# First weights cut in three, first transfers on two queues, and a written order for the first splits

## The chip, the cores and the metric

The kernel runs on one core of one Trainium2 chip. The metric is the device time of one execution in microseconds. Engines are named as in the profile: PE (TensorE), DVE (VectorE), ACT (ScalarE), POOL (GpSimd), and SP, which here only issues DMAs. Each engine works through its own instructions in the order in which they were built, and waits where one needs a result, or a buffer, of another engine.

## The reference

Two layers of a decoder trunk on x with 512 tokens and 1024 features, in float32. The case touches only the start of the first layer's Conformer module:

```python
u = rms_norm(h, conv_norm_g)                    # h = x
a = u @ w_pw1 + b_pw1                           # 1024 -> 2048
u = a[..., :D_MODEL] * jax.nn.sigmoid(a[..., D_MODEL:])
u = causal depthwise convolution of 31 taps(u) + dw_b
h = h + silu(layer_norm(u)) @ w_pw2 + b_pw2
...
def rms_norm(x, g):
    y = xf * lax.rsqrt(jnp.mean(xf * xf, axis=-1, keepdims=True) + EPS)
    return y * g
```

The rest (SwiGLU, a gated input embedding, differential attention with its own SwiGLU and embedding) is the same code before and after.

## The kernel before

**Layout.** x is held transposed: eight chunks h0 to h7 of 128 features by 512 tokens (256 KB each). A product with a weight is taken in three matmuls, so that float32 comes out of the faster rounded format: each operand is split into a rounded upper part ("hi") and the remainder ("lo"), and lo·hi, hi·hi and hi·lo are summed (`mm3`, lines 163 to 168). A weight tile is 128 x 1024 (512 KB) and holds all eight blocks of 128 x 128 that one chunk of 128 outputs needs. `weight()` (147 to 161) loads it with a DMA from SP into one of two buffers `wraw`, casts it on ACT into `whi` (159) and subtracts on DVE into `wlo` (161). I number these tiles w0, w1, ... in the order in which they are loaded.

**The norm.** The norm's scale per token is left out of the first product and multiplied in behind it. What the matmuls see is h times the gain, split the same way into a tile `A` of which one half is hi (ACT, 206) and one lo (DVE, 207). Meanwhile ACT squares the eight chunks (237); chunks 0 to 2 are summed over the features on PE by matmuls against ones (199), chunk 3's square is the tile `acc`, into which POOL adds the squares of 4 to 7 (241), and `acc` is summed on PE last. From the sums DVE makes a mean (270), POOL an inverse root (272), DVE a diagonal matrix (277), PE spreads it over the partitions (288, output `tp`), and ACT copies it into the row `rb` (262). All products of this stage are multiplied by `rb`.

**The chunk loop** (500 to 549) makes the 16 x 128 outputs in eight chunks. Each takes a gate half and a value half, 24 matmuls of 128 x 512 each, in accumulators `mm`, of which there are four in rotation: chunk 2's gate half writes the one that chunk 0's gate half used. DVE multiplies both halves by `rb` (523, 529), which frees the accumulators; ACT takes the sigmoid (524, with a table load ahead of it), DVE joins the two (541, or 533 for chunks 1, 3, 5, 6, which goes on by DMA through DRAM, 370 and 374, to convolution taps on PE at 407). The taps of chunks 0, 2 and 4 run on DVE (453, 455, 458) and, as products of ACT summed by POOL, on those two (442, 445, 446). Each chunk also loads the next chunk's two weights, so w2 and w3 serve chunk 1, w4 and w5 chunk 2, w6 and w7 chunk 3. Between w5 and w6 two halves of the input p use the same two `wraw` buffers (312 to 314; ACT casts, POOL subtracts). A buffer's next transfer is issued by SP when its cast and its subtraction are done, so w4 follows w2, p's first half follows w4, and w6 follows p's first half.

**The order** of the instructions on each engine is set by the building program's scheduler, except where the code binds it (`issue_after`, and `manual_schedule` for whole blocks). The first two weights come in two halves each, with the first chunks of x between them on SP's queue (lines 299 to 307). Only `vec`, a table of gains and biases, comes by ACT's queue (120).

Of the kernel before, what the change touches and what calls it, by code (L numbers as in the profile page):

```python
# [13 lines left out]
F32R = mybir.dt.float32r  # L14
# [32 lines left out]


SHIFT = 1
WARM = 9  # L50
ALONE = (7,)
CUTS = 2

# [38 lines left out]
def trunk(ctx, tc, xT, pT, wts, diag, dww, vec, rel, onehot, lamv, out):  # L92
# [9 lines left out]
    def sb(shape, tag, bufs, dt=F32):  # L102
        uid[0] += 1
        return pool.tile(shape, dt, tag=tag, name=f"{tag}_{uid[0]}", bufs=bufs)
# [12 lines left out]


    vt = sb([P, 480], "vec", 1)[:, :NV]
    nc.scalar.dma_start(vt, vec)  # L120

    def col(name, i=0):
        a, _ = VEC[name]
# [8 lines left out]
    V.memset(mhalf, -0.5)  # L132
    V.memset(meps, DH * EPS)
    t = wk()[:, 0:P]
    V.memset(t, 1.0)
    V.tensor_copy(ones_r, t)

# [9 lines left out]
    def weight(n=1024, pieces=1, between=(), eng=V, after=(None, None), home=None, parts=None, bufs=1):  # L147
        i = wnext[0]
        wnext[0] += 1
        raw = sb([P, 1024], *(home or ("wraw", 2)))  # L150
        hi = sb([P, 1024], *((parts[0], bufs) if parts else ("whi", 4)), F32R)
        lo = sb([P, 1024], *((parts[1], bufs) if parts else ("wlo", 4)), F32R)
        for k in range(pieces):
            cut = slice(k * n // pieces, (k + 1) * n // pieces)
            loaded[0] = nc.sync.dma_start(raw[:, cut], wts[i, :, cut])
            if k < len(between):
                between[k]()
            with tc.issue_after(after[1].ins) if after[1] else nullcontext():
                A.copy(hi[:, cut], raw[:, cut])  # L159
            with tc.issue_after(after[0].ins) if after[0] else nullcontext():  # L160
                eng.tensor_tensor(lo[:, cut], raw[:, cut], f(hi[:, cut]), ALU.subtract)  # L161
        return hi, lo
# [27 lines left out]
        return t[:, 0], t[:, 1]  # L190


    h = [sb([P, S], f"h{c}", 1) for c in range(NC)]

    def columns_sum(t, src, first, last):

        for b in range(4):
# [11 lines left out]
    class Norm:  # L209
# [18 lines left out]
                self.square = A.activation(sq, h[c], AF.Square)  # L228
                self.last = self.eng.tensor_tensor(self.acc, self.acc, sq, ALU.add)  # L229

        def columns_of_chunks(self, n):

            t = tp()
            acc = sb([P, S], "acc", 1)
            for c in range(NC):
                sq = wk() if c != n else acc
                A.activation(sq, h[c], AF.Square)
                if c < n:
                    columns_sum(t, sq, c == 0, False)
                elif c > n:  # L240
                    G.tensor_tensor(acc, acc, sq, ALU.add)
            columns_sum(t, acc, False, True)
            return rsqrt_cols(first_of(t), 4, 1.0 / D)
# [49 lines left out]


    norm = Norm("conv_g")
    def load(c):
        return lambda: nc.sync.dma_start(h[c], xT[c])

    w0 = weight(pieces=2, between=(load(0),))
    norm.split(0)  # L300
    w1 = weight(pieces=2, between=(load(1), load(2)))
    pair_loads = [loaded[0]]
    pairs = [(w1, w0)]
    for c in range(3, NC):
        load(c)()
    for c in range(1, NC):
        norm.split(c)

    def pfeatures(layer, parts):
        for k, (hi, lo) in enumerate(parts):  # L310
# [189 lines left out]
    for c in range(NC):  # L500
        wa, wg = pairs[c]
        if c == 0:
            pg = half(wg)
            pa = half(wa)
            norm.dg = diagonal(norm.columns_of_chunks(3))
            rb = norm.rows()
        if c + 1 < NC:
            pairs.append((weight(), weight())[::-1])
            pair_loads.append(loaded[0])
        if c == 0:  # L510
            dwt = sb([P, NC * KW], "C4", 2)
            nc.sync.dma_start(dwt, dww)
        if c == 1:
            ph = pfeatures(0, [(sb([P, S], t, 2, F32R), sb([P, S], t, 2, F32R)) for t in ("wth", "wtl")])
        if c > 0:
            pg = half(wg)
            for k in BETWEEN[c]:
                pe_taps(k)
            pa = half(wa)
            for k in BEHIND[c]:  # L520
                pe_taps(k)
        tg, ta = big(), big()
        V.tensor_tensor(tg, pg, rb, ALU.mult)
        gated = A.activation(tg, tg, AF.Sigmoid, bias=col("b_pw1", 8 + c))
        if c == NC - 1:

            with tc.issue_after(gated.ins):
                A.activation(powers[:, 24:32], vt[:, :8], AF.Silu)
        V.tensor_tensor(ta, pa, rb, ALU.mult)
        if c in PHASED:  # L530
            up = big()
            phases, tok = "p (r n) -> p n r", "p (n r) -> p n r"
            V.scalar_tensor_tensor(
                up.rearrange(phases, r=NPH), ta.rearrange(tok, r=NPH), col("b_pw1", c),
                tg.rearrange(tok, r=NPH), ALU.add, ALU.mult,
            )
            phased_in(c, up)
        else:
            up = ups[c] = sb([P, S + PAD], "C0", 2)
            G.memset(up[:, :PAD], 0.0)  # L540
            V.scalar_tensor_tensor(up[:, PAD:], ta, col("b_pw1", c), tg, ALU.add, ALU.mult)
        for k in BETWEEN[c] + BEHIND[c]:
            other_taps(k)
        if c == 1:
            moments(0)
        elif c > 3:
            moments(c - 3)
# [862 lines left out]
```

## Time and profile before

| | us |
|---|---|
| median of 3 runs | 1246.81 (1246.58 to 1248.63) |
| the profiled execution | 1246.42 |
| its span, first to last instruction | 1244.70 |
| around the span | 1.72 |
| PE busy | 1232.4 (99% of the span) |
| DVE, ACT, POOL busy | 882.1, 623.8, 471.1 |

Times in rows of the profile count from the span's start. A row of the timeline gives the start, the length, the engine, the line of the kernel, the operation, output and inputs, how many instructions were merged, and in brackets how long the engine stood idle before it and whose result ended that. "SPq" and "ACTq" are DMA issues of SP and ACT. PE's matmuls overlap, so that one of 0.39 us is followed by the next after 0.23. A float32 matmul with "ones" shows as two passes. "PEclk", the clock that the throttle granted, is full in every slice of the page.

### The profile page before, as it was taken

Reading aid. Unit: us, or ns where it says so; the run is one execution under the profiler, and the core shown is the slowest. Engines: PE = TensorE matmul, PEld = TensorE weight load, DVE = VectorE, ACT = ScalarE, POOL = GpSimd, SP = SyncE. Lnnn points to the kernel's source line nnn. Section 1 sums busy time; section 2 is a strip of 40 time slices with the busy share of each in tenths; the row PEclk is TensorE's granted clock in tenths of the full one; section 3 lists DMA queues with packets and bytes.
Section 4 is the critical chain, followed back from the end, with each engine's and each line's share of the span. In section 5 each row is a group of like instructions: output and inputs, shape, how many; then the busy total and the mean of one; then the engine's idle time right before and its main releaser. Section 6 shows DMA issues by size and latency. Waiting matters only on the chain.

```text
span 1244.7 us, 18430 instructions
## 1 busy us (share of the span) xinstructions
PE 1232.4 (99%) x7080; PEld 1080.8 (87%) x7080; DVE 882.1 (71%) x1242; ACT 623.8 (50%) x1096; POOL 471.1 (38%) x355
## 2 busy tenths in 40 slices
PE   9999999999999999999999999999999999999998
PEld 7888788888998899888888888788889998999887
DVE  6998866885895479547676876646966885587535
ACT  5653464443553255434566877735434552455432
POOL 3863442024670364133346645041026650552120
PEclk9999999999999999999999999999999999999999
DMA  7566213334233322334332331143333333232331
GB/s 267 177 210 193 90 51 119 98 98 127 86 102 118 102 86 71 117 104 149 126 113 76 112 90 38 52 144 93 89 122 95 103 111 112 83 102 86 104 100 67
DMA packets 49154, 136.33 MB, mean 110 GB/s; under 512 B 5635, under 2 KB 10243, under 8 KB 49068
## 3 DMA queue, kind: packets, MB, share of 16 engines
q1 hardware_dynamic: 46944, 131.74, 34.0%
q10 hardware_dynamic: 2124, 3.43, 0.9%
q8 instruction: 55, 0.90, 0.3%
q14 instruction: 31, 0.25, 0.1%
HBM read 128.84 MB, written 6.31 MB: 109 GB/s over the span
## 4 chain that ended last, share of the span: by engine, by line
PE 88%; DVE 4%; issue 2%; DMA 1%; ACT 0%; SPq 0%; POOL 0%; DVEq 0%; ACTq 0%
PE mm L166 27%; PE mm L167 27%; PE mm L168 27%; PE mm L1126 1%; DVE sc L458 1%; PE sc L1094 1%; PE sc L1093 1%; PE tp L1113 1%; PE sc L407 1%; PE mm L407 1%; PE tp L1047 1%; PE mm L363 1%; PE tp L199 1%; DVE wlo L720 0%; DVE wlo L161 0%
## 5 line engine op out<-in xcount | busy, mean ns | idle before, releaser
L159 ACT CAST whi<-wraw 128x1024 fp32r<-128x1024 f32 (+2 forms) x145 | 145.7, 1014 | 229.0 <-PE mm L168 110.9
L161 DVE TENSOR_TENSOR wlo<-wraw,whi 128x1024 fp32r<-128x1024 f32 (+2 forms) x141 | 180.4, 1285 | 82.0 <-ACT whi L159 79.7
L166 PE MATMUL mm<-A,wlo 128*128 128x512 f32 (+1 forms) x568 | 220.4, 388 | 1.1 <-ACT A L206 1.0
L167 PE MATMUL mm<-A,whi 128*128 128x512 f32 (+1 forms) x568 | 219.2, 387 | 0.0
L168 PE MATMUL mm<-A,whi 128*128 128x512 f32 (+1 forms) x568 | 217.3, 389 | 0.0
L166 PE MATMUL mm<-B,wlo 128*128 128x512 f32 x352 | 137.0, 389 | 0.0
L167 PE MATMUL mm<-B,whi 128*128 128x512 f32 x352 | 137.0, 389 | 0.0
L168 PE MATMUL mm<-B,whi 128*128 128x512 f32 x352 | 135.6, 389 | 0.0
L229 POOL TENSOR_TENSOR acc<-acc,wk 128x512 f32<-128x512 f32 x35 | 60.0, 1715 | 190.6 <-ACT wk L228 189.9
L166 PEld LDWEIGHTS mm<-A,wlo 128*128 128x128 f32 x568 | 106.8, 188 | 23.7 <-ACT A L206 1.3
L167 PE MATMUL mm<-C,whi 128*128 128x256 f32 x448 | 126.8, 283 | 0.0
L168 PE MATMUL mm<-C,whi 128*128 128x256 f32 x448 | 126.8, 283 | 0.0
L166 PE MATMUL mm<-C,wlo 128*128 128x256 f32 x448 | 126.8, 283 | 0.0
L168 PEld LDWEIGHTS mm<-A,whi 128*128 128x128 f32 x568 | 106.5, 188 | 21.9 <-issue 0.5
L167 PEld LDWEIGHTS mm<-A,whi 128*128 128x128 f32 x568 | 106.7, 188 | 21.1
L720 DVE TENSOR_TENSOR wlo<-A,whi 128x1024 fp32r<-128x1024 f32 x60 | 106.2, 1778 | 19.7 <-ACT whi L719 19.6
L719 ACT CAST whi<-A 128x1024 fp32r<-128x1024 f32 x60 | 62.9, 1049 | 55.5 <-PE mm L168 44.3
L729 POOL TENSOR_TENSOR A<-A 128x512 f32<-128x512 f32 x16 | 25.7, 1606 | 165.5 <-DMA A<-in_wts 156.7
L729 POOL TENSOR_TENSOR A<-wraw 128x512 f32<-128x512 f32 x16 | 24.7, 1546 | 167.4 <-DMA wraw<-in_wts 152.7
L167 PEld LDWEIGHTS mm<-C,whi 128*128 128x128 f32 x448 | 86.0, 192 | 0.2
L166 PEld LDWEIGHTS mm<-C,wlo 128*128 128x128 f32 x448 | 86.0, 192 | 0.2
L168 PEld LDWEIGHTS mm<-C,whi 128*128 128x128 f32 x448 | 86.0, 192 | 0.0
(314 smaller groups left out, 3031.6 us busy)
## 6 DMA issues: line engine op xcount, KB each, us to landing
wraw<-in_wts SPq DMA_DIRECT2D x161, 512.0 KB, 3.6
A<-in_wts SPq DMA_DIRECT2D x32, 512.0 KB, 3.6
wraw<-in_wts SPq DMA_DIRECT2D x16, 384.0 KB, 3.1
D<-in_diag SPq DMA_DIRECT2D x22, 256.0 KB, 4.8
C<-in_diag SPq DMA_DIRECT2D x16, 256.0 KB, 4.8
h<-in_xT SPq DMA_DIRECT2D x8, 256.0 KB, 5.5
rest<-h SPq DMA_DIRECT2D x8, 256.0 KB, 2.5
bias<-scr ACTq DMA_DIRECT2D x8, 256.0 KB, 3.6
```

The source lines that it names most:

```text
L159: A.copy(hi[:, cut], raw[:, cut])
L161: eng.tensor_tensor(lo[:, cut], raw[:, cut], f(hi[:, cut]), ALU.subtract)
L166: T.matmul(acc, al, bh, start=first, stop=False, **kw)
L167: T.matmul(acc, ah, bh, start=False, stop=False, **kw)
L168: return T.matmul(acc, ah, bl, start=False, stop=last, **kw)
L199: r = T.matmul(t[:, cut], src[:, cut], ones, start=first and b == 0, stop=last and b == 3)
L229: self.last = self.eng.tensor_tensor(self.acc, self.acc, sq, ALU.add)
L363: last_tap[0] = T.matmul(acc, dg[:, j % 4], ups[c][:, j : j + S], start=(j == 0), stop=(j == PE_TAPS[c] - 1))
L407: last_tap[0] = T.matmul(acc[:, g * P : (g + 1) * P], w, ups[c][:, g, LEAD - m : LEAD - m + P], start=(m == 0), stop=(m == LAGS - 1),)
L719: A.copy(hi, src)
L720: V.tensor_tensor(lo, src, f(hi), ALU.subtract)
L729: G.tensor_tensor(s[:, 0], r1[:, 0], r1[:, 1], ALU.add)
```

## The change

It does five things. (1) The tile h0 is issued first on SP, then `vec` on ACT as before, and the warm-up matmuls before the first data are 7 instead of 9. (2) w0 and w1 are cut into pieces of 256, 256 and 512 columns instead of 512 and 512; the first two pieces of w0 are issued from ACT's queue, all else from SP's, with h1, h2 and h3 between the pieces. (3) The casts, subtractions, the eight splits of x and the squares of chunks 0 to 3 stand in a written order for DVE and ACT. (4) The squares of chunks 0 to 3 are passed to the norm's column sums (`squares`), and the others are left to the scheduler. (5) In chunk 0 the gate and value halves are written as one loop over the eight blocks, six matmuls each.

```diff
-WARM = 9
+WARM = 7
...
-    nc.scalar.dma_start(vt, vec)
...
+    h = [sb([P, S], f"h{c}", 1) for c in range(NC)]
+    nc.sync.dma_start(h[0], xT[0])
+    nc.scalar.dma_start(vt, vec)
...
-        def columns_of_chunks(self, n):
+        def columns_of_chunks(self, n, given):
...
-            acc = sb([P, S], "acc", 1)
+            acc = given[n]
             for c in range(NC):
-                sq = wk() if c != n else acc
-                A.activation(sq, h[c], AF.Square)
+                if c in given:
+                    sq = given[c]
+                else:
+                    sq = wk()
+                    A.activation(sq, h[c], AF.Square)
...
-    w0 = weight(pieces=2, between=(load(0),))
-    norm.split(0)
-    w1 = weight(pieces=2, between=(load(1), load(2)))
-    pair_loads = [loaded[0]]
+    pieces = slice(0, 256), slice(256, 512), slice(512, 1024)
...
+    def fetch(i, k, eng):
+        return eng.dma_start(raw2[i][:, pieces[k]], wts[i, :, pieces[k]])
+
+    fetch(0, 0, nc.scalar)
+    fetch(1, 0, nc.sync)
+    fetch(0, 1, nc.scalar)
+    load(1)
+    fetch(1, 1, nc.sync)
+    load(2)
+    fetch(0, 2, nc.sync)
+    load(3)
+    pair_loads = [fetch(1, 2, nc.sync)]
     pairs = [(w1, w0)]
-    for c in range(3, NC):
-        load(c)()
-    for c in range(1, NC):
-        norm.split(c)
+    for c in range(4, NC):
+        load(c)
...
+    with tc.manual_schedule(engines={V.engine, A.engine}):
+        whi(0, 0)
+        wlo(0, 0)
+        norm.split(0)
+        whi(1, 0)
+        norm.split(1)
+        wlo(1, 0)
...
+        norm.split(7)
+        square(3)
...
         if c == 0:
-            pg = half(wg)
-            pa = half(wa)
-            norm.dg = diagonal(norm.columns_of_chunks(3))
+            pg, pa = mm(), mm()
+            for k in range(NC):
+                (gh, gl), (ah, al), (bh, bl) = wpart(wg, k), wpart(wa, k), norm.u[k]
+                T.matmul(pg, gl, bh, start=k == 0, stop=False)
+                T.matmul(pg, gh, bh, start=False, stop=False)
+                T.matmul(pa, ah, bh, start=k == 0, stop=False)
+                T.matmul(pg, gh, bl, start=False, stop=k == NC - 1)
+                T.matmul(pa, ah, bl, start=False, stop=False)
+                T.matmul(pa, al, bh, start=False, stop=k == NC - 1)
+            norm.dg = diagonal(norm.columns_of_chunks(3, squares))
             rb = norm.rows()
```

Where it moves instructions: the scheduler lays out the rest around the written part, and its order differs from before until chunk 4's gate half; from there on all engines have the same order. Three places follow, each as built. In the rows a name's last number tells tiles apart.

On ACT at the start, before (`whi_96` and `whi_109` are the upper parts of w0 and w1, `A_18`, `A_22`, `A_23` the splits of chunks 0 to 2, `wk` their squares):

```order
L120 DMA vec_63<-in_vec 128x99
L159 ACT_TABLE_LOAD
L159 CAST whi_96<-wraw_95 128x512
L206 ACTIVATE A_18_105<-h_7_87,vec_63 128x512
L237 ACTIVATE wk_199<-h_7_87 128x512
L159 CAST whi_96<-wraw_95 128x512
L159 CAST whi_109<-wraw_108 128x512
L206 ACTIVATE A_22_124<-h_8_88,vec_63 128x512
L237 ACTIVATE wk_205<-h_8_88 128x512
L159 CAST whi_109<-wraw_108 128x512
L206 ACTIVATE A_23_127<-h_9_89,vec_63 128x512
```

And now (`whi_96` and `whi_98` are w0 and w1, `A_21` to `A_23` the splits):

```order
L136 DMA vec_63<-in_vec 128x99
L308 DMA wraw_94<-in_wts 128x256 x2
L330 ACT_TABLE_LOAD
L330 CAST whi_96<-wraw_94 128x256
L206 ACTIVATE A_21_117<-h_6_74,vec_63 128x512
L330 CAST whi_98<-wraw_95 128x256
L206 ACTIVATE A_22_121<-h_7_75,vec_63 128x512
L330 CAST whi_96<-wraw_94 128x256
L330 CAST whi_98<-wraw_95 128x256
L206 ACTIVATE A_23_128<-h_8_76,vec_63 128x512
L327 ACTIVATE wk_132<-h_6_74 128x512
```

Two DMA issues came to ACT, the first casts are half as long, and the first square moved behind the splits of chunks 0 to 2.

On PE at the end of chunk 1, before (`mm_316` is chunk 1's value half, `tp_241<-wk_238` the matmul that spreads rb, `A_22` and `A_23` the splits of chunks 1 and 2 of the eight):

```order
L166 MATMUL mm_316<-A_22_124,wlo_252 128x512
L167 MATMUL mm_316<-A_22_124,whi_251 128x512
L288 MATMUL tp_241<-wk_238,ones_70 128x512
L168 MATMUL mm_316<-A_22_124,whi_251 128x512
L166 MATMUL mm_316<-A_23_127,wlo_252 128x512
L167 MATMUL mm_316<-A_23_127,whi_251 128x512
```

And now (`mm_323` is chunk 1's value half, `A_31` the last of the eight splits, `tp_248` the spread row, `mm_432` chunk 2's gate half):

```order
L168 MATMUL mm_323<-A_31_154,wlo_259 128x512
L169 MATMUL mm_323<-A_31_154,whi_258 128x512
L170 MATMUL mm_323<-A_31_154,whi_258 128x512
L291 MATMUL tp_248<-wk_245,ones_69 128x512
L168 MATMUL mm_432<-A_21_117,wlo_275 128x512
```

The spreading matmul moved from inside the value half, with 19 of its matmuls still to come, to its end, directly before chunk 2.

On ACT and DVE behind it, before (ACT, then DVE; `whi_267` and `whi_273` are w4 and w5, `wth` and `wtl` the halves of p, `wlo_415` is w6 and stands further down on DVE):

```order
L159 CAST whi_267<-wraw_266 128x1024
L159 CAST whi_273<-wraw_272 128x1024
L313 CAST wth_278<-wraw_282 128x512
L262 COPY rb_240<-tp_241 128x512
L313 CAST wtl_280<-wraw_286 128x512
L524 ACT_TABLE_LOAD
L524 ACTIVATE big_258<-big_258,vec_63 128x512
```

```order
L270 TENSOR_SCALAR v_42_234<-tp_197 128x4
L277 TENSOR_TENSOR wk_238<-ident_65,r_43_236 128x512
L161 TENSOR_TENSOR wlo_268<-wraw_266,whi_267 128x1024
L161 TENSOR_TENSOR wlo_274<-wraw_272,whi_273 128x1024
L523 TENSOR_TENSOR big_258<-mm_147,rb_240 128x512
L529 TENSOR_TENSOR big_259<-mm_172,rb_240 128x512
L523 TENSOR_TENSOR big_341<-mm_290,rb_240 128x512
```

And now (ACT, then DVE; `whi_421` and `wlo_422` are w6, `whi_427` and `wlo_428` w7, `big_265` is chunk 0's first product with rb):

```order
L161 CAST whi_274<-wraw_273 128x1024
L161 CAST whi_280<-wraw_279 128x1024
L366 CAST wth_285<-wraw_289 128x512
L366 CAST wtl_287<-wraw_293 128x512
L161 CAST whi_421<-wraw_420 128x1024
L265 COPY rb_247<-tp_248 128x512
L161 CAST whi_427<-wraw_426 128x1024
```

```order
L163 TENSOR_TENSOR wlo_275<-wraw_273,whi_274 128x1024
L273 TENSOR_SCALAR v_42_241<-tp_212 128x4
L163 TENSOR_TENSOR wlo_281<-wraw_279,whi_280 128x1024
L280 TENSOR_TENSOR wk_245<-ident_64,r_43_243 128x512
L163 TENSOR_TENSOR wlo_422<-wraw_420,whi_421 128x1024
L583 TENSOR_TENSOR big_265<-mm_162,rb_247 128x512
L589 TENSOR_TENSOR big_266<-mm_163,rb_247 128x512
L583 TENSOR_TENSOR big_348<-mm_297,rb_247 128x512
L589 TENSOR_TENSOR big_349<-mm_323,rb_247 128x512
L163 TENSOR_TENSOR wlo_428<-wraw_426,whi_427 128x1024
```

The copy of rb moved behind the cast of w6 on ACT, and the first product with rb behind the subtraction of w6 on DVE.

31 lines of the change are left out of this document (29 added, 2 removed).

## The prediction

> **What bounds the kernel now.** The page comes first.
>
> ```profile
> span 1244.7 us, 18430 instructions
> PE 1232.4 (99%) x7080; PEld 1080.8 (87%) x7080; DVE 882.1 (71%) x1242; ACT 623.8 (50%) x1096; POOL 471.1 (38%) x355
> ```
>
> TensorE (PE) is busy 99% of the span. A change that adds and removes no matmul that counts can therefore only win or lose by moving the few places where PE waits. All edits lie before 25 us, so I read the timeline there, then on to the next place where PE waits. These are the head and the start of chunk 1:
>
> ```profile
> 0.73 0.38 SPq L155 DMA_DIRECT2D wraw<-in_wts  x1
> 1.17 0.42 SPq L297 DMA_DIRECT2D h<-in_xT  x1
> 1.52 4.21 PE L141 MATMUL tp<-ones,ident 128*128 128x128 f32 x18 [1.52 <-POOL ident masks.py:199]
> 4.03 0.62 ACT L159 CAST whi<-wraw 128x512 fp32r<-128x512 f32 x1 [1.56 <-DMA wraw<-in_wts]
> 5.55 0.58 PE L166 MATMUL mm<-A,wlo 128*128 128x512 f32 x1
> 8.44 0.50 PE L166 MATMUL mm<-A,wlo 128*128 128x512 f32 x1 [0.95 <-ACT A L206]
> 20.62 1.06 PE L199 MATMUL tp<-ones,acc 128*128 128x128 f32 x8
> 21.44 0.48 PE L166 MATMUL mm<-A,wlo 128*128 128x512 f32 x1
> ```
>
> PE warms up until 5.73, starts the real work at 5.55 and idles 0.95 before 8.44. From 5.55 to 21.44 are 15.89 us, for 48 matmuls and four column sums. Here is the border of chunks 1 and 2, with the row of inverse norms (rb) that frees the accumulators of chunk 0:
>
> ```profile
> 28.15 1.02 PE L288 MATMUL tp<-wk,ones 128*128 128x512 f32 x2
> 29.24 0.40 PE L166 MATMUL mm<-A,wlo 128*128 128x512 f32 x1
> 29.46 0.58 ACT L262 COPY rb<-tp 128x512 f32<-128x512 f32 x1
> 30.07 0.69 DVE L523 TENSOR_TENSOR big<-mm,rb 128x512 f32<-128x512 f32 x1 [2.27 <-ACT rb L262]
> 33.14 0.75 DVE L541 SCALAR_TENSOR_TENSOR C<-big,vec,big 128x512 f32<-128x512 f32 x1 [1.18 <-ACT big L524]
> 33.13 0.39 PE L168 MATMUL mm<-A,whi 128*128 128x512 f32 x1
> 33.36 0.39 PE L166 MATMUL mm<-A,wlo 128*128 128x512 f32 x1
> ```
>
> Consecutive matmuls start 0.23 apart (33.13, 33.36), and chunk 2 begins at 33.36 without a gap: the buffer that it writes (there are four) was freed at 30.76, 2.6 us early. That cover is what this case is about. Then come the next place where PE waits, and what leads to it:
>
> ```profile
> 62.95 0.39 PE L168 MATMUL mm<-A,whi 128*128 128x512 f32 x1
> 63.09 0.69 DVE L462 TENSOR_TENSOR B<-sc,wk 128x512 f32<-128x512 f32 x1
> 63.70 0.68 DVE L529 TENSOR_TENSOR big<-mm,rb 128x512 f32<-128x512 f32 x1
> 64.47 2.29 DVE big L533
> 102.95 3.96 DMA C<-pi
> 105.45 0.39 PE L166 MATMUL mm<-A,wlo 128*128 128x512 f32 x1
> 107.58 0.68 PE L407 MATMUL sc<-C,D 128*128 128x128 f32 x4 [1.74 <-DMA C<-pi]
> ```
>
> The rows without a form are from the chain that ended last. Up to 107.58 it runs over VectorE (DVE) and DMAs, and PE, with 1.74 us to spare, waits for it. From there on it is mostly PE. So a delay reaches the end if it gets into DVE's chain at 64.47, and of a delay on PE alone 1.74 us would vanish at 107.58.
>
> **The first transfers and pieces.** The first piece of w0 (128 KB) moves to ScalarE's (ACT's) queue behind vec; SP starts with h0. Bounds for its landing are two landings of before: the first transfer's at 4.03, and the third's,
>
> ```profile
> L155 SPq DMA_DIRECT2D wraw<-in_wts x1: 424/424/424, 1.6 to 1.6; - x1
> DMA to landing us min/median/max: 3.7/3.7/3.7
> ```
>
> issued at 1.64 and landed at 5.34. I take 5.0, nearer the later one: vec (49.5 KB) and h0 (256 KB) go first, and part of h1 beside it. From cast to first matmul before took 5.55 - 4.03 = 1.52; half the cast saves some 0.2, so the first matmul stands at 6.3 (5.4 to 6.7). Chunk 0 needs 15.89 - 0.95 = 14.9 at most from there if nothing waits, so chunk 1 begins at 21.2 instead of 21.44, give or take 1. The two warm-up matmuls fewer cost and save nothing; they ran before any data was there. All this I price at nothing, because of what follows; without that cover it would be 0.2 us won.
>
> The trace shows that SP issues 0.44 us apart (0.73, 1.17), while the transfers issued at 0.73 and 1.64 land 1.31 apart. The Trainium skill, DMA: Bandwidth & Descriptors, section "Issuing engines are not separate DMA queues", says that queues share the same engines and a second one saves only issue time. By that the second queue wins nothing here either, and the trace agrees.
>
> **The order behind it.** This is where the sum is made. In the new order rb's matmul stands after the last matmul of chunk 1 instead of ahead of its last 19; rb's copy on ACT stands behind the cast of w6, and the first product with rb on DVE behind the subtraction of w6. That cast needs w6's transfer, which needs a chain of buffers. The chain as it ran before:
>
> ```profile
> 17.74 1.62 POOL L241 TENSOR_TENSOR acc<-acc,wk 128x512 f32<-128x512 f32 x1
> 16.14 1.98 ACT L159 CAST whi<-wraw 128x1024 fp32r<-128x1024 f32 x2
> 18.13 3.44 DVE L161 TENSOR_TENSOR wlo<-wraw,whi 128x1024 fp32r<-128x1024 f32 x2
> 20.47 1.47 SPq L155 DMA_DIRECT2D wraw<-in_wts  x2
> 24.04 1.05 ACT L159 CAST whi<-wraw 128x1024 fp32r<-128x1024 f32 x1 [5.92 <-DMA wraw<-in_wts]
> 25.13 1.23 DVE L161 TENSOR_TENSOR wlo<-wraw,whi 128x1024 fp32r<-128x1024 f32 x1 [1.41 <-ACT whi L159]
> 26.38 1.77 SPq L312 DMA_DIRECT2D wraw<-in_pT  x2
> 28.93 0.62 ACT L313 CAST wth<-wraw 128x512 fp32r<-128x512 f32 x1 [2.39 <-DMA wraw<-in_pT]
> 29.63 1.30 POOL L314 TENSOR_TENSOR wth<-wraw,wth 128x512 fp32r<-128x512 f32 x1 [6.64 <-ACT wth L313]
> 30.95 1.84 SPq L155 DMA_DIRECT2D wraw<-in_wts  x2
> ```
>
> w2 subtracted, w4 issued (20.47), landed (24.04), subtracted, p issued, landed, split on POOL, w6 issued (30.95). From w4's issue to w6's are 10.48 us.
>
> Where does w4's issue stand now? ACT casts w2 after much the same work: the same elements in two more casts, all eight scalings, two squares fewer (the other two come after w2's cast), begun some 1 us later. So at about 16.2 as before (16.14), done by 17.2. DVE is free then, since POOL's sums now begin only behind the square of chunk 3 (just before w2's cast) and no longer beside the splits; but they run beside w2's subtraction. A subtraction took 1.23 with POOL idle (25.13) and up to this, with POOL at work all through:
>
> ```profile
> 35.49 16.49 POOL L446 TENSOR_TENSOR wk<-wk,C 128x512 f32<-128x512 f32 x9 [3.04 <-ACT C L445]
> 39.05 2.19 DVE L161 TENSOR_TENSOR wlo<-wraw,whi 128x1024 fp32r<-128x1024 f32 x1
> ```
>
> I take 2.19, since POOL has four sums of 1.6 to do: w4 is issued at 19.4 (18.5 with the other price), some 1.1 earlier than before. Then: 10.48 to w6's issue, 3.57 to its landing (20.47 to 24.04), 1.09 to the start of its subtraction (24.04 to 25.13), 1.23 for that, 0.69 for the first product: 17.06 us. PE's chunk 2 starts at 36.4 instead of 33.36, **3.0 us late** (2.1 with the other price; 4.0 if w4's subtraction is doubled as well). Behind w6's subtraction DVE's in-order queue holds all four products and every tap of chunk 0. On SP, w2 and w3 wait until the third pieces are subtracted, and the filter tiles queue behind them; I price that at nothing, since the chunks of x still fill the DMA engines then and PE wants those tiles only in chunk 3.
>
> How much is passed on? DVE starts its products 36.4 - 0.69 - 30.07 = 5.6 late, but one subtraction (39.05, 2.1) is then done already, and the 1.18 wait at 33.14 goes, as the second weight's subtraction fills it: 2.3 late on its own account. At 63.70 it needs chunk 3's second accumulator, whose last matmul ended at 62.95 + 0.39 = 63.34: PE's 3.0, less these 0.36, make it 2.7. That is the larger, and it enters the chain at 64.47, which has its DMAs behind it and brings 2.7 to 107.58. PE alone arrives there 3.0 late, inside its 1.74 plus 2.7. Sum: **+2.7**, on the profiled execution's 1246.42 (span 1244.70 and 1.72 around it) 1249.1. The median of the three runs is 0.39 above that execution, so on its scale 1249.5.
>
> **The rivals.**
>
> *A floor instead of the chain (not slower by what can be told).* If w6 lands 1.5 us sooner, rb alone decides. Its matmul takes the last 0.86 before 33.36 (28.15 to 29.24, less the 0.23 of one matmul between), so starts at 32.5; 1.02 + 0.58 + 0.69 and handovers of 0.1 give 34.9, a stall of 1.5. Less 0.36, and up to 0.8 if the head wins its 0.95, this is +0.3 to +1.2, some 1247.6. For it: w2's subtraction at 1.23 already takes 0.9 off. Against: POOL's four sums must run right there. It decides from a w6 landing at 31.9, where I have 33.4.
>
> *The order pays, and the wait is absorbed.* The head wins its 0.95 and what smaller gaps stand beside it, 1.3 at most; PE's later wait disappears in the 1.74 at 107.58. 1245.5. For it: chunk 0 needs fewer bytes before its first matmuls. Against: DVE's products start at 30.07 before and can't now, and the chain of 64.47 is DVE's.
>
> *POOL becomes the chain.* Its first tap sum moves from 35.49 to 41.5 (products 35.7 to 38.1, a subtraction and the gating until 40.1, two ACT passes): 6.0 late.
>
> ```profile
> 54.07 6.24 POOL L446 TENSOR_TENSOR wk<-wk,C 128x512 f32<-128x512 f32 x4 [2.09 <-ACT C L445]
> 63.09 0.73 ACT L445 ACTIVATE C<-C,C 128x512 f32<-128x512 f32 x1 [0.65 <-POOL wk L446]
> ```
>
> 2.09 are regained at 54.07; ACT's last product at 63.09 waits for POOL and comes 3.9 late, and a weight's cast stands behind it. If this reaches DVE it makes +3.9: 1250.7. It does so where POOL's lag is over about 4.6 at 63; I have 3.9.
>
> *A slow clock at the start.* The 18 warm-up passes take 0.234 each, against 1.06 / 8 = 0.13 for the same shape at 20.62, so PE runs at half pace until about 5.7, 4.2 us after it began. Two passes of four fewer end the warm-up at 4.8, and a pause until 6.3 could start that count anew: 4.2 us at half pace lose 2.1 us of chunk 0. rb's matmul then starts at 34.4 and chunk 2 at 36.8, 0.4 later than forecast: 1249.9. The Trainium skill, TensorE: Matmul & The Clock Gate, "What's actually happening", says that a pause has to last a whole window of about 3.4 us before the clock halves. By that rule a pause of 1.5 us does nothing; no run here has shown such a pause yet.
>
> **How the numbers follow.** What a measurement of this kernel can tell is 0.2%, 2.5 us: slower is above 1249.30, faster below 1244.32. The forecast's mechanism has 0.53; its stall of 2.1 to 4.0 gives 1248.6 to 1250.5, and I put 0.36 of it above 1249.30 and 0.17 below. POOL's chain 0.15 and the clock 0.08 lie above. The floor 0.19 lies below, and so does the absorbed wait, 0.05, of which 0.02 go to faster, as nothing in the profile offers 2.5 us. Slower 0.59, same 0.39, faster 0.02. The likeliest is 1249.5; from the floor's 1247.4 to POOL's 1251.2 should hold eight in ten.
>
> **What would show it.** Right: a PE wait of 2 to 4 us before the first matmul of chunk 2, ended by DVE's first product with rb; ACT's copy of rb directly behind a cast of a landed weight; POOL's first tap sum near 41; PE's wait near 107.58 still there. Wrong in a step: w6 landed well before PE's rb matmul is out (the floor); no wait there at all (rb does not gate); the wait before 107.58 grown (POOL or DVE later than PE); warm-pace matmuls only after 9 us (the clock). The forecast is wrong if chunk 2 starts on PE before 35.

## The result, and the profile after

| | before | after |
|---|---|---|
| median of 6 runs each | 1246.69 | 1253.74 (1252.13 to 1254.50) |
| ratio | | 1.0055, 95% interval 1.0042 to 1.0068 |
| profiled execution, its span | 1246.42, 1244.7 | 1254.46, 1252.6 |

The change makes the kernel 7.05 us slower. The sign and the place were as forecast, the size was not: 2.7 us were expected, 4.4 at the range's end (1251.2 on the scale of 1246.81). The timeline of PE after the change, at the border of chunks 1 and 2:

```profile
33.62 1.02 PE L291 MATMUL tp<-wk,ones 128*128 128x512 f32 x2
38.69 0.79 PE L168 MATMUL mm<-A,wlo 128*128 128x512 f32 x1 [4.04 <-DVE big L583]
39.28 0.63 PE L169 MATMUL mm<-A,whi 128*128 128x512 f32 x1
...
44.40 0.44 PE L169 MATMUL mm<-A,whi 128*128 128x512 f32 x1
44.68 0.39 PE L170 MATMUL mm<-A,whi 128*128 128x512 f32 x1
```

Chunk 2 begins at 38.69 instead of 33.36, 5.33 us late, after a wait for the first product with rb. Behind the wait, matmuls start 0.43 apart instead of 0.23 up to 44.40: 13 distances that take 5.71 us instead of 2.99, 2.7 us more. Together 8.0. The last matmul of chunk 3 starts 8.17 late (71.12 instead of 62.95), and VectorE's product with rb waits for it:

```profile
71.55 0.69 DVE L589 TENSOR_TENSOR big<-mm,rb 128x512 f32<-128x512 f32 x1 [0.70 <-PE mm L170]
72.33 2.04 DVE L593 SCALAR_TENSOR_TENSOR big<-big,vec,big 128x512 f32<-128x512 f32 x1
```

The second row's twin of before stood at 64.47, 7.86 earlier. So what enters VectorE's chain there is PE's lateness. The clock says the same. A row of the windows gives the stretch, the busy time of PE, PEld, DVE, ACT and POOL with their instructions, the mean granted clock (PEclk, the last but two), the busy share of the DMA engines and what they moved in GB/s (the last):

```profile
35.00:40.00 5.00, 1.31 (x3) 1.12 (x4) 3.20 (x5) 2.70 (x4) 0.00 (x0) 0.77 0.69 203
40.00:45.00 5.00, 5.00 (x14) 3.85 (x14) 4.60 (x6) 4.72 (x7) 0.73 (x1) 0.55 0.51 188
```

A mean of 0.77 and then 0.55 means half the clock for 2.3 and for 4.5 us, 37.7 to 44.5. ScalarE's timeline ahead of chunk 2:

```profile
25.14 1.05 ACT L161 CAST whi<-wraw 128x1024 fp32r<-128x1024 f32 x1 [6.41 <-DMA wraw<-in_wts]
35.73 1.04 ACT L161 CAST whi<-wraw 128x1024 fp32r<-128x1024 f32 x1 [3.50 <-DMA wraw<-in_wts]
36.68 0.58 ACT L265 COPY rb<-tp 128x512 f32<-128x512 f32 x1
```

VectorE's in the same stretch:

```profile
36.80 1.23 DVE L163 TENSOR_TENSOR wlo<-wraw,whi 128x1024 fp32r<-128x1024 f32 x1 [6.52 <-ACT whi L161]
37.95 0.68 DVE L583 TENSOR_TENSOR big<-mm,rb 128x512 f32<-128x512 f32 x1
...
41.92 0.75 DVE L601 SCALAR_TENSOR_TENSOR C<-big,vec,big 128x512 f32<-128x512 f32 x1 [0.37 <-ACT big L584]
```

And SyncE's issues, with the time that it took over each:

```profile
11.10 1.21 SPq L157 DMA_DIRECT2D wraw<-in_wts  x2
12.36 0.90 SPq L440 DMA_DIRECT2D D<-in_diag  x2
...
18.53 2.35 SPq L157 DMA_DIRECT2D wraw<-in_wts  x2
```

The spread is out at 34.64, but rb's copy stands behind w6's cast (35.73), and the product behind w6's subtraction. w4 was issued at 18.53 and is cast at 25.14: 6.6 us to land, where before took 3.57. The windows show what moved meanwhile. After the change:

```profile
10.00:15.00 5.00, 5.00 (x29) 4.29 (x28) 3.86 (x6) 5.00 (x10) 0.00 (x0) 1.00 0.84 275
11.00:12.00 1.00, 1.00 (x8) 0.87 (x8) 0.81 (x3) 1.00 (x3) 0.00 (x0) 1.00 0.46 164
15.00:20.00 5.00, 5.00 (x29) 4.26 (x29) 4.00 (x3) 3.73 (x6) 3.98 (x3) 1.00 0.93 339
20.00:25.00 5.00, 5.00 (x24) 4.14 (x23) 0.52 (x1) 0.00 (x0) 2.96 (x2) 1.00 0.98 386
```

The same windows before:

```profile
10.00:15.00 5.00, 5.00 (x31) 4.37 (x30) 3.86 (x6) 5.00 (x10) 2.01 (x2) 1.00 1.04 404
15.00:20.00 5.00, 5.00 (x24) 4.09 (x23) 5.00 (x3) 3.12 (x5) 4.20 (x3) 1.00 0.99 378
20.00:25.00 5.00, 5.00 (x29) 4.29 (x28) 2.43 (x4) 0.96 (x1) 1.03 (x1) 1.00 0.62 212
```

SyncE stood at w2's issue, which waits for a third piece's subtraction, until 11.10, and the nine filter tiles behind it went out at 12.36 to 18.1. The chunks of x kept the DMA engines full until then (a share of 1.03, 395 GB/s, from 10 to 11), and no longer. From 10 to 15 and from 15 to 20 the engines moved 129 and 39 GB/s less than before, 0.84 MB in all; from 20 to 25, while w4 waited, they moved 174 more, 0.87 MB: about the amount that was missed. The later wait of PE, in its timeline below, has shrunk from 1.74 to 0.79 and absorbs 0.95; the row stands 7.2 later than before (the spans end 7.9 apart; where the last 0.7 arise is open):

```profile
114.80 4.26 PE L460 MATMUL sc<-C,D 128*128 128x128 f32 x36 [0.79 <-DMA B<-po]
```

### The profile page after: what moved, and what is told of

The parts are those of the page before. It is cut to its first block, busy times and chain, and to the rows that moved or that the text cites. A ratio compares the mean times of both kernels' runs of the same rounds, so it can differ in the third digit from the quotient of the medians.

```text
span 1252.6 us, 18425 instructions
## 1 busy us (share of the span) xinstructions
PE 1236.9 (99%) x7076; PEld 1083.5 (87%) x7076; DVE 875.8 (70%) x1244; ACT 623.3 (50%) x1098; POOL 468.8 (37%) x355
## 4 chain that ended last, share of the span: by engine, by line
PE 85%; DVE 6%; DMA 3%; issue 3%; ACT 2%; POOL 1%; SPq 1%; DVEq 0%; ACTq 0%; POOLq 0%
PE mm L168 26%; PE mm L169 26%; PE mm L170 26%; DMA wraw<-in_wts 1%; DVE wlo L780 1%; PE sc L460 1%; PE mm L1186 1%; DVE sc L511 1%; PE sc L1154 1%; PE sc L1153 1%; PE mm L460 1%; PE tp L1173 1%; PE tp L1107 1%; PE mm L416 1%; DVE wlo L163 1%
## 5 line engine op out<-in xcount | busy, mean ns | idle before, releaser
L161 ACT CAST whi<-wraw 128x1024 fp32r<-128x1024 f32 (+1 forms) x141 | 143.5, 1025 | 233.8 <-PE mm L170 116.4
L163 DVE TENSOR_TENSOR wlo<-wraw,whi 128x1024 fp32r<-128x1024 f32 (+1 forms) x137 | 178.0, 1305 | 92.9 <-ACT whi L161 92.5
L168 PE MATMUL mm<-A,wlo 128*128 128x512 f32 (+1 forms) x552 | 215.2, 390 | 4.1 <-DVE big L583 4.0
L169 PE MATMUL mm<-A,whi 128*128 128x512 f32 (+1 forms) x552 | 214.9, 389 | 0.0
L170 PE MATMUL mm<-A,whi 128*128 128x512 f32 (+1 forms) x552 | 211.1, 388 | 0.0
L170 PEld LDWEIGHTS mm<-A,whi 128*128 128x128 f32 x552 | 104.2, 189 | 21.6 <-DVE A L674 0.3
L169 PEld LDWEIGHTS mm<-A,whi 128*128 128x128 f32 x552 | 104.4, 189 | 20.9 <-issue 0.2
```

Source lines behind the costliest of these rows:

```text
L168: T.matmul(acc, al, bh, start=first, stop=False, **kw)
L169: T.matmul(acc, ah, bh, start=False, stop=False, **kw)
L170: return T.matmul(acc, ah, bl, start=False, stop=last, **kw)
```

## Experiments

Theory 1: the loss is PE's wait at chunk 2, made longer by the tiles ahead of w4 and by the halved pace behind the pause. Rivals: the head itself (A), GpSimd's and VectorE's chain of taps (B), w4's own transfer (C). All were timed beside the kernel before (1246.08 to 1246.53 in the four sets).

**e1_rb_first**: the splits of w6 and w7 behind rb's copy and the first product.

```diff
-            A.copy(r, spread(self.dg))
+            self.row = A.copy(r, spread(self.dg))
...
-            pairs.append((weight(), weight())[::-1])
+            after = (first_product, norm.row) if c == 2 else (None, None)
+            pairs.append((weight(after=after), weight(after=after))[::-1])
...
```

> The changed kernel, with one thing moved: the casts and subtractions of w6 and w7 stand behind rb's copy on ScalarE and behind the first product with rb on VectorE, not ahead of them. Theory 1 (the loss is PE's 4.04 us at chunk 2's first matmul: rb's copy behind w6's cast, the product behind w6's subtraction, and after this pause 13 matmuls at 0.43 us instead of 0.23): the spread still ends at 34.6, rb's copy 0.6 and the product 0.7 behind it, chunk 2 begins near 36.1 instead of 38.69, PE waits about 1.5 there. If so short a pause leaves PE's pace whole, 2.6 + 2.6 = 5.2 us come back: 1.5 to 3 us over the kernel before instead of 7; if the pace halves again, only 2.6 come back: 4 to 5 us over. Rival A (the head costs: pieces, two queues, the slow first matmuls): the time stays within 1 us of the changed kernel's, about 7 us over the kernel before, since the head is left alone. Rival B (GpSimd's tap sums, 2.8 us late in the changed kernel, set the time): chunk 2 begins earlier, but at least 5 us over stay.

Measured: 1251.30, ratio 1.0041 (1.0029 to 1.0054), 4.9 over. PE at the border of chunks 1 and 2:

```profile
34.30 0.50 PE L168 MATMUL mm<-A,wlo 128*128 128x512 f32 x1 [1.40 <-DVE big L584]
34.63 0.40 PE L169 MATMUL mm<-A,whi 128*128 128x512 f32 x1
```

VectorE behind it, with the gated product of chunk 0 and the twin of the product at 71.55:

```profile
39.29 1.23 DVE L163 TENSOR_TENSOR wlo<-wraw,whi 128x1024 fp32r<-128x1024 f32 x1 [1.80 <-ACT whi L161]
41.33 0.75 DVE L604 SCALAR_TENSOR_TENSOR C<-big,vec,big 128x512 f32<-128x512 f32 x1 [0.81 <-ACT big L587]
...
68.21 0.68 DVE L592 TENSOR_TENSOR big<-mm,rb 128x512 f32<-128x512 f32 x1
```

The wait shrinks to 1.40 and the half pace goes, as theory 1 said, and A as the only cause falls; but more is left than theory 1 allowed. The gated product stands at 41.33, 8.2 us later than before, since w7's split precedes the sigmoids. The product at 68.21 no longer waits for PE, so VectorE's own queue sets it. And PE has waits that neither the kernel before nor the changed kernel has, for the sums that follow the taps (line 546): 0.71 at 135.62 (GpSimd) and 1.11 at 150.66 (VectorE). So B holds a part: theory 2 counts both, PE's wait and the late taps.

**e2_tiles_late**: chunk 1's nine filter tiles behind w5's issue.

```diff
-        return tc.issue_after(pair_loads[c].ins)
+        return tc.issue_after(pair_loads[c + 1 if c == 1 else c].ins)
```

> The changed kernel, with the nine filter tiles of chunk 1 issued behind w5's transfer instead of ahead of w4's; ScalarE's and VectorE's order is the changed kernel's. Theory 1, in the part that says that the filter tiles delayed w4: w4 lands about 3.5 us after its issue instead of 6.5, w6's cast starts near 32.7 instead of 35.73 and is done when the spread ends at 34.6, chunk 2 begins near 36.1, PE's wait there falls from 4.04 to about 1.5, with its pace whole: 1.5 to 3 us over the kernel before. Rival A (the head): no gain, about 7 us over. Rival C (w4's 6.5 us are its own issue and transfer, not the tiles ahead of it): w4 still takes 6 us or more, chunk 2 begins near 38.7, no gain.

Measured: 1253.45, 1.0062 (1.0049 to 1.0075), no gain. ScalarE:

```profile
22.68 1.05 ACT L161 CAST whi<-wraw 128x1024 fp32r<-128x1024 f32 x1 [4.01 <-DMA wraw<-in_wts]
...
30.53 0.62 ACT L366 CAST wth<-wraw 128x512 fp32r<-128x512 f32 x1 [4.31 <-DMA wraw<-in_pT]
...
36.30 1.04 ACT L161 CAST whi<-wraw 128x1024 fp32r<-128x1024 f32 x1 [3.22 <-DMA wraw<-in_wts]
```

w4 came 2.5 earlier, 4.4 behind its issue (18.25) instead of 6.6, so C does not explain most of it; but the tiles now stood ahead of pT, and w6 came no sooner. The test missed its aim.

**e3_warm9** and **e4_before_warm7**: nine warm-ups in the changed kernel (the diff), and seven in the kernel before (its reverse).

```diff
-WARM = 7
+WARM = 9
```

> The changed kernel with 9 warm-up matmuls instead of 7, so that PE does not pause before its first product of chunk 0. If the pause of 0.97 us at 4.87 is what keeps PE at half pace up to 10.3, the half pace now ends near 5.8, and chunk 1 begins near 19.8 instead of 21.70. Theory 1: PE then waits 2 us longer at chunk 2, which begins near 38.7 as before, and the time stays within 0.5 us of the changed kernel's, 7 us over the kernel before. Rival A (the head costs): 2 us less than the changed kernel, 5 us over. If the pause is not the cause, PE keeps half pace to about 10 and nothing moves.

> The kernel before with 7 warm-up matmuls instead of 9: a pause of about 0.7 us before its first product, at 5.5. If a pause while PE is still at half pace keeps it there, as the changed kernel's first microseconds suggest, PE goes at half pace up to about 10.3 instead of 5.7, loses 2 us of chunk 0, and gives most of it back at the wait of 1.74 us at 107.58: 0.3 to 1.6 us over the kernel before. If the half pace ends by the clock's own time since the first matmul, chunk 0 runs as before and nothing changes (within 0.3 us).

Measured: e3 1253.83, 1.0061 (1.0047 to 1.0075); e4 1247.05, 1.0006 (0.9997 to 1.0015), which is no difference that can be told. The head of PE in the changed kernel:

```profile
5.84 0.79 PE L559 MATMUL mm<-A,wlo 128*128 128x512 f32 x1 [0.97 <-ACT A L206]
6.43 0.63 PE L560 MATMUL mm<-A,whi 128*128 128x512 f32 x1
...
9.91 0.60 PE L561 MATMUL mm<-A,whi 128*128 128x512 f32 x1
10.33 0.41 PE L563 MATMUL mm<-A,whi 128*128 128x512 f32 x1
```

The head of PE in e4:

```profile
5.42 0.80 PE L166 MATMUL mm<-A,wlo 128*128 128x512 f32 x1 [0.54 <-ACT A L206]
...
10.71 0.59 PE L166 MATMUL mm<-A,wlo 128*128 128x512 f32 x1
11.13 0.39 PE L167 MATMUL mm<-A,whi 128*128 128x512 f32 x1
```

In these two profiles with 7, PE stayed at half pace for 4 to 5 us more; in e1's, behind a pause of 1.00, it did not. In e3 it went at full pace from its second product, chunk 1 began at 20.46 instead of 21.70, and PE only waited longer at chunk 2, which began no sooner:

```profile
38.57 0.79 PE L168 MATMUL mm<-A,wlo 128*128 128x512 f32 x1 [5.17 <-DVE big L583]
```

A falls: the head is hidden.

**e7_taps_first** and **e8_taps_first_warm9**: as e1, but the splits of w6 and w7 behind chunk 0's gated product (DVE) and ScalarE's first tap; e8 with 9 warm-ups.

```diff
+            after = (gate[0], tap_0[0]) if c == 2 else (None, None)
```

> The changed kernel with the splits of w6 and w7 moved further back than in e1: the casts behind ScalarE's first tap of chunk 0, the subtractions behind chunk 0's gated product on VectorE. In e1 chunk 2 began at 34.30, but the gated product came at 41.33 (33.14 in the kernel before) because w7's cast and subtraction stood ahead of the sigmoids, and 3.6 to 4.9 us were left. Theory 2 (two things are lost: PE's wait at chunk 2, and the chain of taps on VectorE and GpSimd, which starts 8 us late): the gated product comes near 37 to 39, GpSimd's first tap sum near 39 to 41 instead of 43.69, PE's wait at chunk 2 stays near 1.4, and 1 to 3 us over the kernel before are left. Rival (what e1 left is the head, not the taps): 4 to 5 us over, as in e1.

> As e7_taps_first, with 9 warm-up matmuls. PE goes at full pace from its second product of chunk 0 in every run; with 7 it went at half pace up to 10.3 in some and at full pace in others. Theory 2: now that nothing else holds the spread, the 1.7 us that the half pace costs in chunk 0 show: the same as e7 or up to 2 us less, 0.5 to 2.5 us over the kernel before. Rival (the pace in chunk 0 is hidden everywhere): the same as e7 within 0.5.

Measured: e7 1249.88, 1.0028 (1.0016 to 1.0041); e8 1248.74, 1.0022 (1.0013 to 1.0031). The gated product comes at 36.37 in e7 (36.87 in e8), 5 us earlier than in e1, while PE's wait at chunk 2 stays at 1.40, and the time falls by 1.4: B is a part of the cause. (The intervals of e1 and e7 overlap; of their executions, all but one of e7's lie below all but one of e1's.) Between e7 and e8 the intervals overlap too.

**e9_taps_spread_warm9**: e8 with the spread ahead of the fourth step of chunk 1's value half.

```diff
-            pa = half(wa)
+            pa = half(wa, self_spread[0] if c == 1 else None)
```

> As e8_taps_first_warm9, with rb's spread on PE placed in the value half of chunk 1 ahead of its 4th of 8 steps, instead of behind chunk 1. Theory 2: spread near 30, rb near 31, the products of chunk 0 near 31 to 32 (30.07 in the kernel before), chunk 2 on PE without a wait near 33, GpSimd's first tap sum near 37: within 1 us of the kernel before, on either side. Rival (the pieces, the two queues and the interleaving cost something by themselves): 2 us or more over. If chunk 0 begins 0.2 to 0.4 us earlier and this is kept to the end, up to 0.5 us under.

Measured: 1249.62, 1.0023 (1.0014 to 1.0032), a miss. PE reached the spread before its input was there:

```profile
30.75 1.10 PE L293 MATMUL tp<-wk,ones 128*128 128x512 f32 x2 [2.12 <-DVE wk L280]
```

So it is not the place on PE alone that makes rb late, but what comes before the diagonal. GpSimd's sums start from chunk 3's square, which the written order puts last, and end at 23.0 instead of 19.4; and on VectorE the mean stands behind w4's subtraction (27.66, where before it came at 21.72).

**e10_tiles_last**: the changed kernel with the tiles behind w7.

```diff
-        return tc.issue_after(pair_loads[c].ins)
+        return tc.issue_after(pair_loads[c + 2 if c == 1 else c].ins)
```

> The changed kernel with the nine filter tiles of chunk 1 issued behind w7's transfer, behind everything that chunk 2 waits for; e2 had put them behind w5, where they stood ahead of pT, and pT's landing gave back what w4 had won. Theory 1, in the part on the transfers: w4 is cast near 22.7 as in e2, pT lands 3 us after its issue again, w6 is issued near 29.5 and cast near 33, before the spread ends at 33 to 34.6, so rb's copy is not held any more; chunk 2 begins near 36 instead of 38.69, PE waits about 1.5 there, its pace stays whole, and w7's split comes earlier too: 2 to 4.5 us over the kernel before. Rival (the place of the tiles in the queue is of no account, the order on ScalarE alone decides): chunk 2 near 38.7, 7 us over.

Measured: 1253.04, 1.0052 (1.0040 to 1.0065). w4 was cast at 22.70 and w6 at 33.39 as expected, but with the casts so early the scheduler put rb's copy behind w7's too:

```profile
33.39 1.04 ACT L161 CAST whi<-wraw 128x1024 fp32r<-128x1024 f32 x1 [3.69 <-DMA wraw<-in_wts]
35.97 1.04 ACT L161 CAST whi<-wraw 128x1024 fp32r<-128x1024 f32 x1 [1.54 <-DMA wraw<-in_wts]
36.92 0.58 ACT L265 COPY rb<-tp 128x512 f32<-128x512 f32 x1
```

Two things had changed at once, so nothing follows for what the tiles cost in time. (w4's landing can be read all the same: 4.5 us from its issue at 18.22.)

**e11_fill**: ten matmuls that nobody reads, between chunk 1's value half and chunk 2.

```diff
+                for k in range(10):
+                    filler = T.matmul(t[:, 0:P], ident, ones, start=True, stop=True)
```

> The changed kernel with 10 matmuls of 128x128 put on PE behind rb's spread; their results are overwritten. They fill about 2.2 us of PE's wait at chunk 2, so that no pause there is longer than 2 us; the order of some taps further on moves too. If the pause of 4 us is what halves PE's pace (0.43 us a matmul instead of 0.23 for about 6.8 us), the first 13 matmuls of chunk 2 now go at 0.23, chunk 2 still begins near 38.7, and PE is 2.6 us earlier behind it; of this 1 to 2.6 us reach the end, if the chain of taps, which starts as late as before, does not hold them: 4.5 to 6.5 us over the kernel before. If the pace is halved for another reason than the pause, the 13 matmuls stay at 0.43 and the time near 7 us over.

Measured: 1258.97, 1.0099 (1.0085 to 1.0114), a miss. The scheduler moved taps, and PE met a new wait of 4.50 at 66.45. Nor was the pause filled, as this run's head was at full pace and the spread earlier:

```profile
32.82 2.39 PE L576 MATMUL sc<-ones,ident 128*128 128x128 f32 x20
39.00 0.79 PE L168 MATMUL mm<-A,wlo 128*128 128x512 f32 x1 [3.79 <-DVE big L595]
...
41.72 0.56 PE L168 MATMUL mm<-A,wlo 128*128 128x512 f32 x1
42.12 0.39 PE L169 MATMUL mm<-A,whi 128*128 128x512 f32 x1
```

It tells one thing: after 3.79 us of pause the half pace lasted 3.1 us, not 5.7.

**e12_tiles_taps**: e8 with the tiles behind w7, by e10's line.

> e8_taps_first_warm9 with the filter tiles of chunk 1 behind w7's transfer, so that the transfers' place is changed and the order on ScalarE is not (in e10 rb's copy also fell behind w7's cast, which hid what the transfers were worth). Theory 2 (the late landing of w4 costs only where rb's copy and the first product stand behind w6's split): w4 is cast near 22.7 instead of 25.5 and w6 near 41 as before, chunk 2 begins near 35.2, the same time as e8 within 0.7 us, 1.5 to 3 us over the kernel before. Rival (the gap in the transfers costs by itself): 1.5 us or more below e8.

Measured: 1249.74, 1.0025 (1.0017 to 1.0033), which overlaps e8's interval. w4 was cast at 22.42, 3.65 behind its issue. Where rb does not stand behind w6, the late w4 costs nothing that can be told.

**e13_squares**: e12 with chunk 3's square written second, and columns, spread and factor of rb earlier (the factor ahead of w4's subtraction).

```diff
-        square(1)
+        square(3)
...
+            after = (gate[0], tap_0[0]) if c == 2 else (last_v[0], None) if c == 1 else (None, None)
...
-            pg = half(wg)
+            pg = half(wg, columns_last[0] if c == 1 else None, 2)
...
-            pa = half(wa)
+            pa = half(wa, self_spread[0] if c == 1 else None, 4)
```

> e12_tiles_taps, with the whole path to rb earlier: the square of x chunk 3, which GpSimd's sums start from, is written second of the four and not last; the sum of squares on PE stands ahead of the third step of chunk 1, the spread ahead of the fifth step of its value half, and rb's column factor on VectorE ahead of w4's subtraction. Theory 2 (all that is left is rb's lateness, through the chain of taps): spread near 28 to 29, rb near 29.5 to 30.3 (29.46 in the kernel before), chunk 2 begins near 32 without a wait (33.36), the gated product near 33.5 (33.14): within 1 us of the kernel before, and up to 1 us under it if PE's earlier start is kept. Rival (the interleaving, the pieces or the written order cost something that rb does not show): 1.5 us or more over.

Measured: 1245.96, 0.9995 (0.9987 to 1.0004). The loss is back within what can be told, with pieces, queues and interleaving kept, and the written order but for the squares. Against the changed kernel the warm-up matmuls, the place of the tiles, the splits of w6 and w7 and the path to rb have all moved, so e13 doesn't divide the loss among them. PE has no wait ahead of chunk 2, the gated product comes at 34.34, and rb's copy, expected near 30, at 31.69:

```profile
31.69 0.58 ACT L265 COPY rb<-tp 128x512 f32<-128x512 f32 x1
```

**e14_one_queue**: e8 with w0's first two pieces on SyncE's queue.

```diff
-    fetch(0, 0, nc.scalar)
+    fetch(0, 0, nc.sync)
...
-    fetch(0, 1, nc.scalar)
+    fetch(0, 1, nc.sync)
```

> e8_taps_first_warm9 with the two pieces of the first weight that ScalarE's queue issued put on SyncE's queue, ahead of x chunk 1: one queue issues all first transfers. If the second queue saves only issue time, x chunk 0 still comes first, the first product of chunk 0 starts at 5.8 to 6.8 instead of 5.78, and the time is that of e8 plus 0 to 1 us. If two queues move more at a time, the first product comes at 7 or later and the time is 1 us or more over e8.

Measured: 1249.34, 1.0024 (1.0016 to 1.0033), which overlaps e8's interval. The first product even starts earlier, at 5.15 (5.78 in e8): w0's first piece is now issued at 1.17, where e8 issues h1. PE then waits 0.44 and 0.47 for what comes later. The second queue is worth nothing that can be told.

**e15_tiles_last_w7**: e10 with w7's cast behind rb's copy, so that the tiles alone change place ahead of chunk 2 (some taps further on move too).

```diff
-            pairs.append((weight(), weight())[::-1])
+            pairs.append((weight(), weight(after=(None, norm.row) if c == 2 else (None, None)))[::-1])
```

> The changed kernel with the filter tiles of chunk 1 behind w7's transfer, as in e10, but with rb's copy between the casts of w6 and w7, where the changed kernel has it (in e10 it fell behind w7's cast). Theory 1, in the part on the transfers: w4 is cast near 22.7, w6 near 33.4, rb's copy follows at 34.4, w6's subtraction ends at 35.7, and chunk 2 begins near 36.4 instead of 38.69; the pause is near 2.8 us, shorter than the 3.0 after which the granted clock fell in the runs so far, so PE's pace stays whole: the changed kernel less 2 to 4 us, 3 to 5 us over the kernel before. Rival (where the tiles stand costs nothing, as the prediction had it): within 1 us of the changed kernel, 7 us over.

Measured: 1249.61, 1.0035 (1.0023 to 1.0048), so moving the tiles takes away about half of the loss, 3.5 of 7.05; no execution took longer than the shortest of the changed kernel (1252.13). How it does so, this run's profile shows only in part. The profiled execution was the slowest of the five (1252.13). ScalarE's cast of w4, and PE:

```profile
24.16 1.05 ACT L161 CAST whi<-wraw 128x1024 fp32r<-128x1024 f32 x1 [5.60 <-DMA wraw<-in_wts]
34.10 1.10 PE L291 MATMUL tp<-wk,ones 128*128 128x512 f32 x2 [1.79 <-DVE wk L280]
37.65 0.79 PE L168 MATMUL mm<-A,wlo 128*128 128x512 f32 x1 [2.45 <-DVE big L583]
38.24 0.63 PE L169 MATMUL mm<-A,whi 128*128 128x512 f32 x1
```

Chunk 2 began at 37.65, not at 36.4 as expected: w4 took 6.0 us from its issue (18.15) though no tile stood ahead of it, against 4.4 and 4.5 in e2 and e10, and why is open. Nor did the pace stay whole. The mean clock of this execution was 0.996; two of the five had 0.999 and 1.000 and took 1248.91 and 1249.03: the same kernel, 3 us apart with the clock.

**e16_early**: e13 with the diagonal ahead of w5's subtraction, rb's copy and the first sigmoid ahead of pT's casts, the spread ahead of chunk 1's value half.

```diff
-            pairs.append((weight(after=after), weight(after=after))[::-1])
+            later = (dg_0, None) if c == 1 else after
+            pairs.append((weight(after=after), weight(after=later))[::-1])
...
-            pg = half(wg, columns_last[0] if c == 1 else None, 2)
+            pg = half(wg, columns_last[0] if c == 1 else None, 3)
...
-            pa = half(wa, self_spread[0] if c == 1 else None, 4)
+            pa = half(wa, self_spread[0] if c == 1 else None, 0)
```

> e13_squares with rb two to three us earlier still: the sum of squares ahead of the fourth step of chunk 1's gate half and the spread ahead of its value half, the diagonal ahead of w5's subtraction, rb's copy and the first sigmoid ahead of pT's casts. Theory 2 (rb's lateness was all that was lost; PE sets the time once rb is early): rb near 28 to 29 (29.46 in the kernel before, 31.69 in e13), the gated product of chunk 0 near 31 to 32.5 (33.14; 34.34 in e13), chunk 2 near 32.5 (33.36): 0.3 to 2 us under the kernel before. Rival (something of the change costs beside rb, and e13 sits at its floor): the time of e13, within 0.3 us, or more.

Measured: 1244.82 against 1246.08 in the same set, 0.9991 (0.9982 to 1.0000). It is 1.3 us under the kernel before, with an interval that touches no difference, and so some 8 (7.05 and 1.26) under the changed kernel. ScalarE's copy of rb:

```profile
28.07 0.59 ACT L265 COPY rb<-tp 128x512 f32<-128x512 f32 x1 [1.77 <-PE tp L295]
```

VectorE's gated product:

```profile
30.73 0.75 DVE L612 SCALAR_TENSOR_TENSOR C<-big,vec,big 128x512 f32<-128x512 f32 x1 [0.15 <-ACT big L595]
```

## Why the prediction was right in kind and wrong in size

**The head.** The first product of chunk 0 came at 5.84 (forecast 6.3, bounds 5.4 to 6.7). Chunk 1 began at 21.70 instead of 21.2, as the clock rival came true there: half pace to 10.33. "Cost and save nothing" was wrong of the two warm-ups by 1.2 us of chunk 0 in the executions profiled (21.70 against 20.46 in e3), and right of the whole, since the wait hid it. That the second queue wins nothing held (e14).

**The step that failed** is the one on SyncE: the filter tiles behind w2 and w3, "I price that at nothing, since the chunks of x still fill the DMA engines then and PE wants those tiles only in chunk 3". It asked who wants the tiles, not who stands behind them. The x chunks filled the engines only until 11 us, and the tiles were still moving when w4 was queued: its landing took 6.6 instead of the 3.57 taken from before. With the tiles out of its way it took 4.4 and 4.5 (e2, e10), but 6.0 in e15's profile, so that not all of the 6.6 is shown to be the tiles. Moving them alone is worth 3.5 us (e15).

**The rest of the chain** held to 0.1: from w4's cast to chunk 2 13.55, forecast 36.4 - 19.4 - 3.57 = 13.43. w4's issue came at 18.53 instead of 19.4, where the lower price of the subtraction had it, and that was partly luck: w2's cast was done at 16.72 (forecast 17.2), and its subtraction took 1.53, between the two prices (1.23 and 2.19). So chunk 2 is 2.3 later than forecast: 3.0 more for the landing, 0.9 less for the issue, 0.1 for the rest, rounded.

**A missing term**: the clock behind the wait. The clock was weighed only at the start; the forecast's own stall was taken to cost its length. It cost 2.7 more here; e15's five executions, at clocks of 0.996 to 1.000, differ by 3.2. The Trainium skill, TensorE: Matmul & The Clock Gate, "What's actually happening", says that the gate looks at free-running windows of about 3.4 us. The traces agree: full pace began at 10.33, the half clock at 37.7 and ended at 44.5, eight windows and two windows of 3.41 later, and in e2, e3, e10 and e15 the half clock lasted 6.8 as well, in e11 3.4. That a pause must last a whole window, as the prediction read the page, is too strict: the window that ended at 37.7 held some 0.4 us of matmuls (the spread's end, at 34.64), and in e15, where the clock fell at 36.2, the 3.41 us ahead of that held the whole spread of 1.1.

**What was passed on.** That PE's 0.36 of slack at chunk 3 come off held: PE was 8.17 late and VectorE's row 7.86. The wait at 107.58 is still there, as forecast, but of its 1.74 only 0.79 are left, where the forecast's numbers leave 1.4 (1.74 + 2.7 - 3.0): PE itself was later than VectorE's chain.

**The rivals.** The floor fell: w6 was cast at 35.73, not at 31.9. GpSimd's chain was not what set the time after the change, though its lag was 8.8, not 6.0, as its rows show (44.27 against 35.49 before), and at 63 still 6.3 (69.39 against 63.14), over the 4.6 that the rival named: PE was later still, VectorE's product at 71.55 waited for PE, and e1 gains as PE's wait shrinks. But the taps are the next bound: 4.9 us remain in e1 until they come first (e7) and rb comes early (e13, e16).

```profile
44.27 7.66 POOL L499 TENSOR_TENSOR wk<-wk,C 128x512 f32<-128x512 f32 x5 [10.67 <-ACT C L498]
...
69.39 1.29 POOL L499 TENSOR_TENSOR wk<-wk,C 128x512 f32<-128x512 f32 x1
```

**What stays open**: how the 7.05 divide exactly among pause, pace and taps, as each edit moved two of them; how much of w4's 6.6 us the tiles make; and whether e16 is really under the kernel before.

## What to carry to other kernels

A step moved ahead of or behind others must be followed down the queue of everything it issues: a transfer that nobody wants yet still stands ahead of one that somebody does. A stall of PE can cost more than its length: here one of 1.40 (e1) left the pace whole, while those of 3.79 to 5.29 lost 1.5 to 2.7 us more to the half pace behind them (e11, e3). And a value that frees a buffer (rb) should not be queued behind work that waits for a transfer.

## What the runs showed of the hardware

The start of full pace differs between kernels whose first microseconds are built alike: with 7 warm-up matmuls three of eight profiled kernels kept half pace to between 9.5 and 11.1 (the changed kernel, e2, e4), five were at full pace from the second product on (e1 at 6.12). With 9, all eight were. That the number of warm-ups decides it is not shown: the pauses ahead of the first product were 0.97 and 1.02 us in two of the slow ones and 0.91 to 1.15 in the five others. The trace's clock column shows 1.00 in those slow first microseconds; only the distance of the matmuls, 0.43 against 0.23, shows the pace.
